# One gathered row in six is summed on GpSimd, with a descriptor ring of 4 KB

## The chip, the core and the metric

The kernel runs on one core of a Trainium2 chip. Its engines work side by side, each through its own queue in order: TensorE (PE in the profile, its weight loads PEld), VectorE (DVE), ScalarE (ACT), GpSimd (POOL) and SyncE (SP). Data moves between memory and the on-chip buffers through 16 DMA engines. The metric is the time of one execution on the device in microseconds (us).

## What is computed

Two layers of a decoder over 256 tokens of width 1024. Each layer mixes the tokens (four groups: short convolution, latent attention, conformer convolution, windowed attention), and then sends each token through PEER, a layer that picks 16 of 16384 experts for each of 8 heads. Cut to what matters here:

```python
def peer_ffn(x, w_q, sub_keys, u_tab, v_tab):
    ...
        gate = jax.nn.softmax(best_s, axis=-1).astype(xc.dtype)
        u = u_tab[idx]
        act = jax.nn.gelu(jnp.einsum('chkd,cd->chk', u, xc), approximate=False)
        vsel = v_tab[idx]
        return jnp.einsum('chk,chkd->cd', gate * act, vsel)

def reference(...):
    for l in range(DEPTH):
        ...
        h = layer_norm(ALPHA * x + mix @ w_out[l], ln1_g[l], ln1_b[l])
        x = layer_norm(ALPHA * h + peer_ffn(h, ...), ln2_g[l], ln2_b[l])
```

Every token needs 8 x 16 = 128 rows of u and of v, in float32; a row of u and one of v lie side by side in memory, 8 KB together.

## The kernel before

The tokens are two tiles of 128, one token to a partition. With two layers that makes four phases, (l, t) = (0,0), (0,1), (1,0), (1,1). A phase is the function `peer`: 128 steps k, one for each expert of a token. A step gathers one "row" tile (line 760: 128 tokens x 2048 floats, 1 MB, an indirect DMA issued by GpSimd into one of `ROWS` = 10 buffers), multiplies its u half with h and sums it up on VectorE (line 763, below "the product"), and the function `post` of the step before does the rest: gelu and gate on ScalarE (lines 745, 746), a 128x128 diagonal matrix `dg` from the result (line 748), and two matrix products of dg with the v half into `acc`, two PSUM banks that collect the sum over all 128 rows (line 750). When the last of these has read a row buffer, it is free for a later gather. `finish` adds ALPHA * h to acc (line 774) and does the layer norm.

While the rows of one phase run, other work is fed in between by `paced`: the mixer of the next tile (`mixer`, which ends with the products of w_out, line 585) and the routing that finds the experts of later heads (`route`). A step of `peer` is put out first, at high priority, then as much of the tasks as their share of `cost` says; `keep_behind` ties the tasks' instructions to steps a few slots back. So each engine has one fixed order in which row steps and tasks alternate. The last phase has no mixer beside it. Weights come through SyncE's queue (`load_w`); from the second mixer on, the four w_out pieces are loaded into row buffers (`w_out_rows` with a tile of tag "row"), which gathers can't use meanwhile.

Gathers land on eight semaphores that are used in turn, so the gather of row k+8 waits for the landing of row k, besides waiting for its buffer.

In the first mixer, 23 taps of a convolution are added on GpSimd (line 505), beside taps on VectorE (line 509).

Of the kernel before, what the change touches and what calls it, by code (L numbers as in the profile page):

```python
# [11 lines left out]
F32 = mybir.dt.float32  # L12
# [3 lines left out]
AF = mybir.ActivationFunctionType  # L16
ALU = mybir.AluOpType
AX = mybir.AxisListType

P = 128  # L20
DM = 1024
# [6 lines left out]
ALPHA = (2 * L) ** 0.25  # L28
# [20 lines left out]

ORDER0 = [1, 3, 0, 2]  # L50
ORDER = [3, 0, 2, 1]

TAPS = 24

# [10 lines left out]
def kernel(ctx: ExitStack, tc: tile.TileContext, x, positions, w_in, w_att, bcast, perch, lnrows, lncols,  # L65
                      w_out, w_qk, uv, ident, mla_mask, swa_dist, iota, invf, out):
    nc = tc.nc
    cp = ctx.enter_context(tc.tile_pool(name="cp", bufs=1))
    lp = ctx.enter_context(tc.tile_pool(name="lp", bufs=1))
# [9 lines left out]
    V, S = nc.vector, nc.scalar  # L79
# [62 lines left out]
    def layer_norm(dst, src, r, store=None, gb=None):  # L142

        mean, rstd = norm_stats(src, DM)
        yield 2.4
        for j in range(2):
            sl = slice(j * 512, (j + 1) * 512)
            if gb is not None:
                g, b = gb[:, sl], gb[:, DM + j * 512:DM + (j + 1) * 512]
            else:  # L150
                g, b = (pm.tile([P, 512], F32, tag="mm", name="lnp") for _ in range(2))
                for i, ps in enumerate((g, b)):
                    for k in range(4):
                        p = (r + i) * KC + j * 4 + k
                        nc.tensor.transpose(ps[:, k * P:(k + 1) * P], rows[:, p:p + 1].to_broadcast([P, P]), idn)
            V.scalar_tensor_tensor(src[:, sl], src[:, sl], mean, g, op0=ALU.subtract, op1=ALU.mult)  # L156
            V.scalar_tensor_tensor(dst[:, sl], src[:, sl], rstd, b, op0=ALU.mult, op1=ALU.add)
            if store is not None:
                nc.sync.dma_start(store[:, sl], dst[:, sl])
            yield 1.5  # L160
# [128 lines left out]
    def mixer(l, t, y, xt):  # L289
# [273 lines left out]
        hp = None  # L563
        order = ORDER0 if start else ORDER

# [168 lines left out]
        yield 0.5  # L734

    R, held, HT = {}, {}, {}

    def peer(l, t, h, acc):

        n = NH * TOPK  # L740
        order = HEADS[t]
        prev = None

        def post(k, act, row, gate):
            S.activation(act, act, AF.Gelu)  # L745
            S.activation(act, act, AF.Copy, scale=gate[:, k % TOPK:k % TOPK + 1])  # L746
            dg = gp.tile([P, P], F32, tag="dg", name="dg", bufs=3)
            S.activation(dg, idn, AF.Copy, scale=act)  # L748
            for j in range(2):
                nc.tensor.matmul(acc[j], dg, row[:, DM + j * 512:DM + (j + 1) * 512],  # L750
                                 start=(k == 0), stop=(k == n - 1))

        for k in range(n):
            while (l, t, order[k // TOPK]) not in R:
                yield None
            ix8, ix, gate = R[l, t, order[k // TOPK]]
            if ix8 is not None and k % TOPK < 8:
                ix = ix8
            row = gp.tile([P, 2 * DM], F32, tag="row", name="row")
            nc.gpsimd.indirect_dma_start(out=row, out_offset=None, in_=uv,  # L760
                                         in_offset=bass.IndirectOffsetOnAxis(ap=ix[:, k % TOPK:k % TOPK + 1], axis=0))
            act = gp.tile([P, 1], F32, tag="act", name="act", bufs=3)
            V.scalar_tensor_tensor(row[:, :DM], row[:, :DM], 1.0, h, op0=ALU.mult, op1=ALU.mult, accum_out=act)  # L763
            if prev is not None:
                post(*prev)
            prev = (k, act, row, gate)
            yield 1
        post(*prev)

    def finish(l, t, h, acc):  # L770
        hp = mp.tile([P, DM], F32, tag="S", name="hp2")
        for j in range(2):
            sl = slice(j * 512, (j + 1) * 512)
            V.scalar_tensor_tensor(hp[:, sl], h[:, sl], ALPHA, acc[j], op0=ALU.mult, op1=ALU.add)
        yield 1.2
        xo = xp.tile([P, DM], F32, tag="x", name=f"x{t}_{l}")
        yield from layer_norm(xo, hp, 4 * l + 2, out[t * P:(t + 1) * P, :] if l == L - 1 else None)
        X[t] = xo
# [175 lines left out]
```

## Time and profile before

| | before |
|---|---|
| time, median of 3 runs | 1524.01 us (1522.01 to 1524.16) |
| profiled execution, its own time | 1520.93 us |
| its span, first to last instruction | 1518.9 us |
| TensorE busy | 1336.2 us, 88% |
| VectorE busy | 1096.7 us, 72% |
| GpSimd busy | 632.3 us, 42% |
| ScalarE busy | 590.1 us, 39% |
| moved by DMA | 614.47 MB, mean 405 GB/s |

Busy times are shares of the whole span. Matrix products are pipelined, and a busy TensorE is not one at its peak. "DMA share" in the tables below is the mean share of time in which the 16 DMA engines had a packet in work; it comes out at up to 1.01 or 1.02. "Idle before" gives the time an engine waited ahead of an instruction, and what released it. The profiled execution is one run; its time lies 3.1 us below the median.

### The profile page before, as it was taken

What the parts mean: (1) busy time and instruction counts of PE and PEld (TensorE: products, weight loads), DVE (VectorE), ACT (ScalarE), POOL (GpSimd) and SP (SyncE); (2) the same over time, 40 slices, a digit from 0 to 9 for tenths busy, and PEclk for the clock granted to TensorE, in tenths of its full rate; (3) what the DMA queues carried; (4) which work ended last, traced back from release to release, by engine and by line L of the source; (5) the groups of instructions that cost most, each with busy time, mean ns of one, the idle gap of its engine ahead of it and who ended that gap; (6) DMA issues with size and microseconds to landing.
All of it is one profiled execution on the core that took longest, in us unless ns stands there. A gap on an engine that the chain in (4) does not pass through costs nothing.

```text
span 1518.9 us, 17527 instructions
## 1 busy us (share of the span) xinstructions
PE 1336.2 (88%) x4852; PEld 714.6 (47%) x4852; DVE 1096.7 (72%) x3161; ACT 590.1 (39%) x2047; POOL 632.3 (42%) x539
## 2 busy tenths in 40 slices
PE   8999979988989997889998989889998888888876
PEld 8576534444436653444445555544544433333222
DVE  5778887588767668876877667876887766676545
ACT  4233443334433324443343333542344334333332
POOL 2034333444554343444454333224355454655551
PEclk9999999999999999999999999899999999999999
DMA  9489999999999999999999999989999999999995
GB/s 383 177 324 426 426 428 396 385 401 424 426 426 427 426 426 427 420 389 426 427 427 426 427 426 427 411 334 407 419 426 428 426 427 426 427 427 427 427 427 220
DMA packets 86208, 614.47 MB, mean 405 GB/s; under 512 B 10336, under 2 KB 10720, under 8 KB 12768
## 3 DMA queue, kind: packets, MB, share of 16 engines
q0 software_dynamic: 73728, 536.90, 84.7%
q1 hardware_dynamic: 12096, 76.44, 12.3%
q8 instruction: 40, 0.66, 0.2%
q14 instruction: 56, 0.46, 0.1%
q10 hardware_dynamic: 288, 0.01, 0.0%
HBM read 612.26 MB, written 1.05 MB: 404 GB/s over the span
## 4 chain that ended last, share of the span: by engine, by line
PE 41%; DMA 31%; DVE 17%; ACT 5%; issue 4%; POOL 0%; DVEq 0%; POOLq 0%; SPq 0%; ACTq 0%
DMA row<-in_uv_dram,ix 31%; PE acc L750 24%; DVE row L763 7%; PE ps_q L680 6%; PE ps_o L585 3%; DVE cv L509 2%; ACT dg L748 1%; PE ps_cfa L319 1%; PE ps_mla L323 1%; ACT act L746 1%; PE ps_rs L685 1%; PE ps_scb L319 1%; ACT act L745 1%; PE po L284 1%; ACT L265 1%
## 5 line engine op out<-in xcount | busy, mean ns | idle before, releaser
L750 PE MATMUL acc<-row,dg 128*128 128x512 f32 x2048 | 977.9, 612 | 152.2 <-ACT dg L748 147.1
L760 POOL DMA_INDIRECT row<-in_uv_dram,ix x512 | 621.1, 1213 | 830.0 <-PE acc L750 272.5
L763 DVE SCALAR_TENSOR_TENSOR row<-row,h 128x1024 f32<-128x1024 f32 x512 | 619.2, 1219 | 217.2 <-DMA row<-in_uv_dram,ix 177.3
L750 PEld LDWEIGHTS acc<-row,dg 128*128 128x128 f32 x2048 | 364.1, 192 | 638.2 <-ACT dg L748 325.0
L745 ACT ACTIVATE act<-act 128x1 f32<-128x1 f32 x512 | 103.5, 202 | 586.2 <-DVE row L763 582.5
L748 ACT ACTIVATE dg<-idn,act 128x128 f32<-128x128 f32 x512 | 205.6, 402 | 24.8 <-PE acc L750 9.6
L746 ACT ACTIVATE act<-act,gate 128x1 f32<-128x1 f32 x512 | 150.2, 294 | 16.2 <-DVE gate L732 1.1
L680 PEld LDWEIGHTS ps_q<-hT,w_q_t 128*128 128x128 f32 x1024 | 124.1, 192 | 28.9 <-issue 27.3
L680 PE MATMUL ps_q<-hT,w_q_t 128*128 128x128 f32 x1024 | 126.9, 275 | 3.9 <-DVE hp L156 3.5
L509 DVE SCALAR_TENSOR_TENSOR cv<-cfu,pc,cv 128x128 f32<-128x128 f32 x217 | 67.6, 359 | 0.9
L585 PE MATMUL ps_o<-w_out_t,mT 128*128 128x512 f32 x128 | 60.9, 618 | 1.7 <-DVE mT L373 1.7
L655 DVE MAX8 tv<-rsc 128x8 f32<-128x128 f32 x64 | 18.5, 290 | 53.1 <-ACT rsc L687 47.5
L687 ACT COPY rsc<-ps_rs 128x128 f32<-128x128 f32 x64 | 17.0, 265 | 94.4 <-PE ps_rs L685 89.5
L683 ACT COPY rq<-ps_q 128x128 f32<-128x128 f32 x64 | 16.6, 259 | 66.2 <-PE ps_q L680 66.1
L763 DVE DVE_READ_ACCUMULATOR row<-row,h 128x1 f32 x512 | 42.2, 82 | 0.0
L585 PEld LDWEIGHTS ps_o<-w_out_t,mT 128*128 128x128 f32 x128 | 24.7, 198 | 31.0 <-issue 28.2
L685 PEld LDWEIGHTS ps_rs<-w_q_t,rq 128*128 128x128 f32 x128 | 22.9, 190 | 25.5 <-issue 20.9
L685 PE MATMUL ps_rs<-w_q_t,rq 128*128 128x128 f32 x128 | 24.7, 277 | 2.8 <-DVE hp L156 1.7
L323 PE MATMUL ps_mla<-w_in_t,xT 128*128 128x208 f32 x128 | 25.8, 353 | 0.6 <-ACT xT L118 0.5
L323 PEld LDWEIGHTS ps_mla<-w_in_t,xT 128*128 128x128 f32 x128 | 23.5, 199 | 3.9 <-issue 2.2
L649 DVE TENSOR_TENSOR grid<-tf,ab 128x512 f32<-128x512 f32 (+1 forms) x33 | 22.3, 674 | 0.6
L650 DVE TENSOR_REDUCE ex<-grid 128x32 f32<-128x512 f32 (+1 forms) x33 | 22.1, 671 | 0.6
(215 smaller groups left out, 958.7 us busy)
## 6 DMA issues: line engine op xcount, KB each, us to landing
w_in_t<-in_w_in_dram SPq DMA_DIRECT2D x24, 1024.0 KB, 9.5
w_q_t<-in_w_qk_dram SPq DMA_DIRECT2D x20, 1152.0 KB, 9.1
w_out_t<-in_w_out_dram SPq DMA_DIRECT2D x16, 1024.0 KB, 6.2
row<-in_uv_dram,ix POOLq DMA_INDIRECT x512
w_in_t<-in_w_in_dram SPq DMA_DIRECT2D x6, 832.0 KB, 8.7
att<-in_w_att_dram SPq DMA_DIRECT2D x2, 640.0 KB, 13.1
x<-in_x_dram SPq DMA_DIRECT2D x2, 512.0 KB
gb<-in_lnrows_dram SPq DMA_DIRECT2D x1, 1024.0 KB
```

Of the source, the lines that this page charges most:

```text
L319: nc.tensor.matmul(ps, w[:, c, j * P:(j + 1) * P], xT[:, c, :], start=(c == 0), stop=(c == KC - 1))
L323: nc.tensor.matmul(ps, xT[:, c, :], w[:, c, a:b], start=(c == 0), stop=(c == KC - 1))
L509: V.scalar_tensor_tensor(cv[j], src, wt, cv[j], op0=ALU.mult, op1=ALU.add)
L585: nc.tensor.matmul(po[j], mixed_T()[:, 2 * g + c, :], wg[:, c, j * 512:(j + 1) * 512], start=(n == 0 and c == 0), stop=(n == 3 and c == 1))
L680: nc.tensor.matmul(ps, wq[:, c, j * P:(j + 1) * P], hT[:, c, :], start=(c == 0), stop=(c == KC - 1))
L685: nc.tensor.matmul(ps, qT, w[:, KC * 256 + j * P:KC * 256 + (j + 1) * P], start=True, stop=True)
L745: S.activation(act, act, AF.Gelu)
L746: S.activation(act, act, AF.Copy, scale=gate[:, k % TOPK:k % TOPK + 1])
L748: S.activation(dg, idn, AF.Copy, scale=act)
L750: nc.tensor.matmul(acc[j], dg, row[:, DM + j * 512:DM + (j + 1) * 512], start=(k == 0), stop=(k == n - 1))
L760: nc.gpsimd.indirect_dma_start(out=row, out_offset=None, in_=uv, in_offset=bass.IndirectOffsetOnAxis(ap=ix[:, k % TOPK:k % TOPK + 1], axis=0))
L763: V.scalar_tensor_tensor(row[:, :DM], row[:, :DM], 1.0, h, op0=ALU.mult, op1=ALU.mult, accum_out=act)
```

## The change

In the phases (0,0), (0,1) and (1,0) each phase has a tile `side` of 128x1024. At step 5 ScalarE fills it with ALPHA * h. For the steps k = 9, 15, 21 and so on up to 123, `post` makes no dg and no matrix product: ScalarE scales the v half of the row in place (128x1024), and GpSimd adds it to `side`. `finish` then adds side and acc, in place of ALPHA * h and acc. The phase (1,1) stays as it was. The ring in which GpSimd writes the descriptors of its DMAs takes 4096 bytes of each partition; without the argument it takes 16384.

```diff
+SIDE = (6, 9)
...
+    SUM = {(0, 0): None, (0, 1): None, (1, 0): None}
...
+        aside = (l, t) in SUM
+
         def post(k, act, row, gate):
             S.activation(act, act, AF.Gelu)
             S.activation(act, act, AF.Copy, scale=gate[:, k % TOPK:k % TOPK + 1])
+            if aside and k >= SIDE[1] and (k - SIDE[1]) % SIDE[0] == 0 and k < n - 4:
+                v = row[:, DM:2 * DM]
+                S.activation(v, v, AF.Copy, scale=act)
+                nc.gpsimd.tensor_tensor(SUM[l, t], SUM[l, t], v, op=ALU.add)
+                return
             dg = gp.tile([P, P], F32, tag="dg", name="dg", bufs=3)
...
+            if aside and k == 5:
+
+                SUM[l, t] = lp.tile([P, DM], F32, tag="side", name="side")
+                S.activation(SUM[l, t], h, AF.Copy, scale=ALPHA)
             if prev is not None:
                 post(*prev)
...
-            V.scalar_tensor_tensor(hp[:, sl], h[:, sl], ALPHA, acc[j], op0=ALU.mult, op1=ALU.add)
+            if (l, t) in SUM:
+                V.tensor_tensor(hp[:, sl], SUM[l, t][:, sl], acc[j], op=ALU.add)
+            else:
+                V.scalar_tensor_tensor(hp[:, sl], h[:, sl], ALPHA, acc[j], op0=ALU.mult, op1=ALU.add)
...
-    nc = _bacc.Bacc("TRN2", target_bir_lowering=False, num_devices=1)
+    nc = _bacc.Bacc("TRN2", target_bir_lowering=False, num_devices=1, dynamic_dma_scratch_size=4096)
```

Lines of the kernel move with it: 750 becomes 760, 760 becomes 770, 763 becomes 773, 585 becomes 587; the new copy is line 754, the new add line 755.

GpSimd's order in the first phase, with the semaphores that each instruction waits for (DMASW0 to 7 are the landings of gathers; row_1204 is the row of k = 9, the last gather above the add is that of k = 17). Before:

```order
L760 DMA row_1358<-in_uv_dram,ix_1034 128x2048 [waits DMASW0_49,DVE_49,PE_49]
L760 DMA row_1399<-in_uv_dram,ix_1034 128x2048 [waits DMAHW4_49,DMASW1_49,PE_49]
L760 DMA row_1420<-in_uv_dram,ix_1034 128x2048 [waits DMASW2_49,DVE_49,PE_49]
L760 DMA row_1440<-in_uv_dram,ix_1034 128x2048 [waits DMASW3_49,DVE_49,PE_49]
L760 DMA row_1473<-in_uv_dram,ix_1034 128x2048 [waits DMASW4_49,DVE_49,PE_49]
```

The same place in the changed kernel:

```order
L770 DMA row_1358<-in_uv_dram,ix_1034 128x2048 [waits DMASW0_49,DVE_49,PE_49]
L770 DMA row_1397<-in_uv_dram,ix_1034 128x2048 [waits DMAHW4_49,DMASW1_49,PE_49]
L755 TENSOR_TENSOR side_1118<-side_1118,row_1204 128x1024 [waits Activation_49]
L770 DMA row_1418<-in_uv_dram,ix_1034 128x2048 [waits DMASW2_49,DVE_49,PE_49]
L770 DMA row_1438<-in_uv_dram,ix_1034 128x2048 [waits DMASW3_49,DVE_49,Pool_49]
L770 DMA row_1471<-in_uv_dram,ix_1034 128x2048 [waits DMASW4_49,DVE_49,PE_49]
```

The add of row k = 9 now stands between the gathers of k = 17 and k = 18 and waits for ScalarE; the gather of k = 19, which takes the buffer of k = 9, waits for GpSimd's own add in place of TensorE. The other 59 adds stand in much the same way, four to seven gathers apart from the next in most places.

TensorE's order near the end of the first phase's mixer, between the third and the fourth w_out group (ps_o). Before:

```order
L750 MATMUL acc_925<-row_2441,dg_2457 128x512
L750 MATMUL acc_926<-row_2441,dg_2457 128x512
L750 MATMUL acc_925<-row_2451,dg_2483 128x512
L750 MATMUL acc_926<-row_2451,dg_2483 128x512
L685 MATMUL ps_rs_2573<-w_q_t_2487,rq_2571 128x128
L750 MATMUL acc_925<-row_2477,dg_2505 128x512
L750 MATMUL acc_926<-row_2477,dg_2505 128x512
L750 MATMUL acc_925<-row_2499,dg_2516 128x512
L750 MATMUL acc_926<-row_2499,dg_2516 128x512
L750 MATMUL acc_925<-row_2510,dg_2535 128x512
L750 MATMUL acc_926<-row_2510,dg_2535 128x512
L585 MATMUL ps_o_2298<-w_out_t_2526,mT_1939 128x512 x2
```

The same place in the changed kernel:

```order
L760 MATMUL acc_925<-row_2425,dg_2441 128x512
L760 MATMUL acc_926<-row_2425,dg_2441 128x512
L687 MATMUL ps_rs_2555<-w_q_t_2469,rq_2553 128x128
L760 MATMUL acc_925<-row_2461,dg_2487 128x512
L760 MATMUL acc_926<-row_2461,dg_2487 128x512
L760 MATMUL acc_925<-row_2481,dg_2498 128x512
L760 MATMUL acc_926<-row_2481,dg_2498 128x512
L760 MATMUL acc_925<-row_2492,dg_2517 128x512
L760 MATMUL acc_926<-row_2492,dg_2517 128x512
L587 MATMUL ps_o_2284<-w_out_t_2508,mT_1931 128x512 x2
```

Five rows stood there and four stand there now; the routing product and the w_out group keep their places.

## Rows read from the trace of the kernel before

**Rows 1.** Busy time by stretch: span, engines (instructions), TensorE's clock, DMA share, GB/s.

```profile
88.00:228.00 140.00, 126.49 (x578) 78.86 (x576) 122.72 (x431) 60.24 (x208) 55.94 (x51) 0.98 0.99 418
228.00:361.00 133.00, 120.76 (x414) 62.54 (x415) 95.61 (x279) 47.66 (x174) 54.05 (x47) 1.00 0.99 398
361.00:608.00 247.00, 218.52 (x830) 121.14 (x829) 179.08 (x506) 96.75 (x338) 106.47 (x86) 0.98 1.01 426
608.00:684.00 76.00, 66.65 (x230) 34.63 (x229) 59.86 (x187) 34.88 (x120) 30.36 (x26) 0.96 1.00 404
684.00:969.00 285.00, 256.36 (x945) 139.82 (x944) 206.34 (x574) 109.31 (x380) 119.49 (x102) 0.98 1.01 426
969.00:1045.00 76.00, 69.82 (x255) 37.74 (x254) 58.76 (x192) 32.73 (x109) 22.70 (x23) 1.00 0.93 363
...
1121.00:1482.00 361.00, 309.01 (x840) 132.42 (x840) 241.56 (x562) 142.70 (x504) 196.51 (x148) 1.00 1.01 427
```

The engines in these rows are, in order, PE, PEld, DVE, ACT, POOL.

**Rows 2.** From the page: engines' busy time over the span, and GpSimd's DMA queue.

```profile
PE 1336.2 (88%) x4852; PEld 714.6 (47%) x4852; DVE 1096.7 (72%) x3161; ACT 590.1 (39%) x2047; POOL 632.3 (42%) x539
...
q0 software_dynamic: 73728, 536.90, 84.7%
```

**Rows 3.** The first gather (timeline: start, length), and line 763: ns min/median/max, first start.

```profile
88.39 1.09 POOL L760 DMA_INDIRECT row<-in_uv_dram,ix  x1 [52.20 <-issue]
...
L763 DVE SCALAR_TENSOR_TENSOR row<-row,h x512: 1194/1220/1301, 94.0 to 1504.9; 128x1024 f32<-128x1024 f32 x171
```

**Rows 4.** GpSimd's largest wait: 228 to 361, 608 to 684, 969 to 1045 us.

```profile
POOL row L760 <- PE acc L750: 27.5, 18, 3.2
...
POOL row L760 <- PE acc L750: 18.6, 11, 3.6
...
POOL row L760 <- PE acc L750: 19.6, 9, 5.6
```

**Rows 5.** From the page's costliest groups: busy us, mean ns, idle before.

```profile
L750 PE MATMUL acc<-row,dg 128*128 128x512 f32 x2048 | 977.9, 612 | 152.2 <-ACT dg L748 147.1
```

**Rows 6.** ScalarE's groups, each shape apart: busy us, mean ns, idle before.

```profile
L748 ACT ACTIVATE dg<-idn,act 128x128 f32<-128x128 f32 x512 | 205.6, 402 | 24.8 <-PE acc L750 9.6
L746 ACT ACTIVATE act<-act,gate 128x1 f32<-128x1 f32 x512 | 150.2, 294 | 16.2 <-DVE gate L732 1.1
L745 ACT ACTIVATE act<-act 128x1 f32<-128x1 f32 x512 | 103.5, 202 | 586.2 <-DVE row L763 582.5 <-issue 3.2
...
L118 ACT COPY xT<-ps_xT 128x512 f32<-128x512 f32 x5 | 2.9, 586 | 15.9 <-PE ps_xT L125 15.8
...
L451 ACT COPY sq<-ps_swq 128x256 f32<-128x256 f32 x4 | 1.4, 362 | 1.5 <-PE ps_swq L319 1.5
```

**Rows 7.** Small adds on GpSimd; VectorE's step beside them, then behind them (ns min/median/max).

```profile
L505 POOL TENSOR_TENSOR cv<-cv,tap x23: 454/457/621, 23.5 to 35.7; 128x128 f32<-128x128 f32 x23
...
L509 DVE SCALAR_TENSOR_TENSOR cv<-cfu,pc,cv x22: 352/499/607, 23.0 to 35.8; 128x128 f32<-128x128 f32 x22
...
L509 DVE SCALAR_TENSOR_TENSOR cv<-cfu,pc,cv x15: 345/348/353, 36.4 to 42.1; 128x128 f32<-128x128 f32 x15
```

**Rows 8.** Timeline of the steady state in the last phase: product, gather, next product.

```profile
1440.32 1.23 DVE L763 SCALAR_TENSOR_TENSOR row<-row,h 128x1024 f32<-128x1024 f32 x1 [1.24 <-DMA row<-in_uv_dram,ix]
...
1440.98 1.37 POOL L760 DMA_INDIRECT row<-in_uv_dram,ix  x1 [1.10 <-DMA row<-in_uv_dram,ix]
...
1442.76 1.23 DVE L763 SCALAR_TENSOR_TENSOR row<-row,h 128x1024 f32<-128x1024 f32 x1 [1.21 <-DMA row<-in_uv_dram,ix]
```

**Rows 9.** Timeline: two gathers beside VectorE's product, one behind its start, one ahead.

```profile
399.26 1.22 DVE L763 SCALAR_TENSOR_TENSOR row<-row,h 128x1024 f32<-128x1024 f32 x1
...
399.57 1.72 POOL L760 DMA_INDIRECT row<-in_uv_dram,ix  x1 [0.30 <-DVE tm L725]
...
403.40 0.94 POOL L760 DMA_INDIRECT row<-in_uv_dram,ix  x1 [0.30 <-issue]
...
403.47 1.23 DVE L763 SCALAR_TENSOR_TENSOR row<-row,h 128x1024 f32<-128x1024 f32 x1 [1.18 <-DMA row<-in_uv_dram,ix]
```

## The prediction

> **What bounds the kernel now.** I read the stage table first (busy time of each engine by stretch, with DMA share and GB/s), since a share over the whole span hides which stage is short of what. Between 361 and 608, 684 and 969, and 1121 and 1482 us the DMA engines are taken at a share of 1.01 and move 426 to 427 GB/s [rows 1]: a ceiling, held for 893 us while TensorE is busy 86 to 90% and VectorE 67 to 73%. TensorE's 88% of the span [rows 2] is therefore not the bound there: work taken off it in those stretches buys nothing. The reader is to look for the stretches below the ceiling. There are three behind the filling of the queue: 398 GB/s over 133 us, 404 over 76 us, 363 over 76 us [rows 1]. Against 427 they lose 29/427 x 133 = 9.0 us, 23/427 x 76 = 4.1 us and 64/427 x 76 = 11.4 us, together 24.5 us. Up to 88 us no gather runs [rows 3], and behind 1482 us the last rows drain; neither stretch is edited. So 24.5 us is about all that this edit can win, 1.6% of the time.
>
> Then I read the waits of GpSimd in these three stretches, because it issues the gathers: its largest is for TensorE's acc matmuls of line 750, 27.5, 18.6 and 19.6 us [rows 4]. That wait is for a row buffer. It fits the code: here the second half of the mixer borrows row buffers for w_out_t, and TensorE works through mixer, routing and row matmuls in one order.
>
> **The change, part by part.** Per phase k = 9, 15, ... 123 go aside: 20 rows, 60 in three phases.
>
> *Taken off TensorE.* One row's two products into acc appear as four MATMULs; 2048 of them are busy 977.9 us [rows 5], so 977.9/512 = 1.91 us a row, 60 x 1.91 = 115 us in all. What counts is what lies in the three stretches. They issue 47, 26 and 23 gathers or so (the instruction counts of POOL in [rows 1]), one in six aside: 8, 4 and 4, sixteen rows, 16 x 1.91 = 30.6 us. The excerpt from TensorE's order shows it: five rows between two w_out groups become four, and nothing else changes place. I count half of it, 15.3 us. TensorE is 91, 88 and 92% busy there [rows 1], so time taken from it does come forward, but part of it turns into waiting for the softmax and norm chains that the mixer runs on other engines.
>
> *Put on ScalarE.* A 128x128 dg (402 ns) gives way to a 128x1024 copy in place. Copies of 256 and 512 columns took 362 and 586 ns [rows 6], 0.875 ns a column; 402 + 896 x 0.875 = 1.19 us, so 0.79 us more a row, 47 us over 60 rows, and three begin-copies of 1.19 us. ScalarE is 36 to 46% busy in the three stretches [rows 1]; its free time hides this. Without that cover the next row's dg would come 0.8 us later.
>
> *Put on GpSimd.* The trace has GpSimd adds of 128x128 only: 457 ns [rows 7]. Were it all fixed cost, 128x1024 would take 0.46 us; were it all by column, 8 x 457 = 3.7 us. If as much of it is fixed as on VectorE (348 ns for 128 columns [rows 7], 1230 for 1024 [rows 8], so 222 ns fixed), 235 ns remain for 128 columns and the whole is 2.1 us. I take 2.5 us, between the last two and nearer to the one made from a step of the same kind.
>
> *The wait that comes with it.* In GpSimd's order the add of row k stands behind the gather of row k+8 and ahead of that of row k+9 (first excerpt). Queued behind it are all later gathers. Let row k's product on VectorE start at 0. In the steady state the gather of k+8 starts 0.66 us later, released by a landing, since eight landing semaphores are used in turn; the next is due 2.44 us on, at 3.1 us [rows 8]. The add can start when product, gelu, gate and copy are done, 1.2 + 0.2 + 0.3 + 1.2 and some gaps = 3.1 us [rows 6, 8], and ends at 5.6 us, or up to 6.8 us if it must first let a product pass. So one gather in six is 2.5 to 3.7 us late, and the two after it catch up, since a free gather takes 0.94 us [rows 9] and one is due each 2.44 us. Eight gathers of 2.44 us are some 19.5 us of work in hand, against 5.6 us from a first gather to its first product (88.4 to 94.0 us [rows 3]). So at the ceiling I cost this at nothing: the queue of landed and flying rows hides it. In the three stretches that queue is short and 3 us may show; but there the buffers are late already, and a row that goes aside no longer waits in TensorE's order. I set these two against each other.
>
> *VectorE against GpSimd.* This is the cost that can decide. In [rows 9] the gather of 399.57 us starts 0.31 us into a product of VectorE and takes 1.72 us; the one of 403.40 us starts 0.07 us ahead of a product and takes 0.94, the product 1.23 as ever. So the one that comes second waits. And while the 23 small adds ran, VectorE's two-input step over 128 columns took 499 ns, and 348 ns right behind them [rows 7]: 151 ns more for an add of 457 ns. By columns, 8 x 151 = 1.2 us a side row; below, nothing, if the add finds VectorE idle; above, the whole add, 2.5 us. I take 1.2 us: sixteen rows, 19 us of VectorE time in the three stretches. VectorE has 37, 16 and 17 us free there [rows 1] for 9.6, 4.8 and 4.8 us. I count a quarter as late in the first two (3.6 us) and all in the third (4.8 us), where the DMA engines fall furthest below the ceiling and a late product is felt at once. That is 8.4 us.
>
> The Trainium skill's page "SBUF — State Buffer", section "Who interferes with whom", speaks against this change: a VectorE instruction with two SBUF inputs and a GpSimd instruction that reads SBUF share a port pair, the pair is an exclusive lock, and whichever comes second is blocked until the first is done. The gathers agree with it; the small adds show a third of an add's length, not all of it. By the page's reading the 19 us would be 40 us.
>
> *The ring, and the rest.* A gather leaves 73728/512 = 144 packets [rows 2], 9 on each of 16 DMA engines, and the landing semaphores let eight gathers fly: 72 packets per engine. The trace has no ring size, so it cannot say when 4 KB is short; I cost it at nothing and keep a rival for it. The Trainium skill's "DMA: Bandwidth & Descriptors", section "Terms", gives a descriptor as 16 bytes; by that, and one descriptor a packet (an estimate), 4 KB would hold 256, and the sum would stay as it is; no run here shows it. The last step of a phase reads the side sum in place of h, the same shape: nothing.
>
> **The sum.** -15.3 + 8.4 = -6.9 us. The profiled execution took 1520.9 us (span 1518.9 and 2.0 around it): 1514.0. It lies 3.1 us below the median of the runs shown, so on the median: 1524.0 - 7 = **1517 us**.
>
> **The rivals.**
> (1) *The lock costs more than TensorE gives* (slower). The whole add blocks VectorE: 16 x 2.5 = 40 us in the three stretches. It decides once the blocking is above what VectorE has free around each add. Between 88 and 228 us VectorE has 140 - 122.7 = 17.3 us free [rows 1] for 7 adds, 17.5 us: just full. If half of the 40 us shows, +20 - 15 = +5, 1529 us; if all, 1549 us. For it: the gathers of [rows 9]. Against: the small adds of [rows 7], and VectorE's free fourth.
> (2) *No change.* The three stretches are short because the mixer holds buffers, not because TensorE is full; what TensorE saves it waits out. 1524 us. For it: other waits of GpSimd there, and the ceiling in the rest of the span. Against: [rows 4].
> (3) *All of the shortfall comes back*, since the relief, 30.6 us, is above the 24.5 us lost: 1499.5 us. Against: the third stretch loses 11.4 us and gets only 4 x 1.91 = 7.6 us.
> (4) *The ring is too small.* If it let only two gathers fly, a row would take 5.6/2 = 2.8 us in place of 2.44: 512 x 0.36 = 184 us more, about 1708 us. Against: [rows 2], 9 packets an engine.
>
> **How the numbers follow.** Forecast (a gain of 3 to 15 us) 0.46, rival 3 0.12, rival 2 0.18, rival 1 0.20, rival 4 0.04. Within 0.2%, 3 us, is about what a measurement of this kernel can't tell from no change. Faster 0.46 + 0.12 = 0.58, same 0.18, slower 0.24. For eight in ten I leave out the outermost part of rival 3, the upper end of rival 1 and rival 4: 1502 to 1533 us; below, 22 of the 24.5 us; above, 9 us, a little past rival 1 at half.
>
> **What would show it.** TensorE's busy time down by some 115 us (1336 to 1221) with the span almost the same is the plainest sign that it did not bound. The three stretches should show 402 to 415 GB/s; if one stays or falls and VectorE's products of line 773 there are longer or start later, rival 1 is at work. An add of 128x1024 should take 2.1 to 3.0 us; above 3.7 its cost was wrongly built up. If GB/s falls below 420 between 361 and 608 us, the late gathers are not hidden, or the ring is short; the waits of GpSimd tell which.

## Result, and the profile after

The changed kernel takes 1558.58 us (median of five runs, 1557.2 to 1561.01); the kernel before took 1522.01 us beside it (1516.62 to 1524.16). The ratio is 1.0244 with a 95% interval of 1.0229 to 1.026: 37 us slower. The forecast was 1517 us and the range ended at 1533. The profiled execution took 1561.01 us, with a span of 1559.2 us against 1518.9 before.

The stage table of the changed kernel: stretch, its length, busy time (and instructions) of PE, PEld, DVE, ACT and POOL, TensorE's clock, DMA share, GB/s. Its rows answer to [rows 1]; a row for 1045 to 1121 us is added.

```profile
88.00:228.00 140.00, 118.03 (x549) 75.25 (x547) 125.90 (x409) 56.85 (x187) 69.32 (x54) 0.94 0.98 402
228.00:361.00 133.00, 109.55 (x375) 57.65 (x376) 102.67 (x255) 56.37 (x181) 65.75 (x51) 0.92 0.94 375
361.00:608.00 247.00, 202.50 (x769) 114.16 (x767) 197.47 (x499) 102.20 (x332) 135.62 (x101) 0.93 1.01 420
608.00:684.00 76.00, 54.55 (x160) 28.68 (x160) 64.76 (x196) 35.02 (x102) 34.08 (x26) 0.80 0.94 356
684.00:969.00 285.00, 242.50 (x888) 133.69 (x889) 222.98 (x533) 115.59 (x373) 157.36 (x118) 0.95 1.01 422
969.00:1045.00 76.00, 55.83 (x205) 30.82 (x204) 62.68 (x215) 37.30 (x105) 26.75 (x22) 0.84 0.83 321
1045.00:1121.00 76.00, 68.71 (x249) 37.55 (x250) 58.18 (x134) 31.13 (x104) 43.98 (x34) 0.98 1.00 412
1121.00:1482.00 361.00, 301.50 (x844) 133.56 (x842) 264.40 (x628) 147.85 (x511) 210.44 (x153) 0.98 1.01 423
```

No stretch gained, every one lost. Against 427 GB/s the time lost is (427 - GB/s)/427 x length: 8.2, 16.2, 4.0, 12.6, 3.3, 18.9, 2.7 and 3.4 us, together 69.3. By the same sum the rows of before [rows 1] lose 2.9, 9.0, 0.6, 4.1, 0.7, 11.4, 0.7 (423 GB/s from 1045 to 1121 us) and nothing, together 29.4. The difference, 39.9 us, is the whole difference of the spans, 40.3 us. By these rows 23.2 us of it lie in the three stretches that the prediction wanted to shorten.

But the windows stand still while the program falls behind, by some 27 us at 969 us, so a line of this table is not the same work as its line of before. The stretches can be cut instead where the trace of the changed kernel has moved as many bytes as the kernel before at the edges of [rows 1]. Cut so, the first is 9.9 us longer than before and the three wanted ones 2.7, 11.4 and 9.6 us (23.7 together):

```profile
88.00:237.90 149.90, 122.41 (x557) 77.31 (x555) 133.74 (x427) 63.54 (x204) 72.99 (x57) 0.91 0.96 390
237.90:373.60 135.70, 111.63 (x382) 57.62 (x380) 107.26 (x280) 54.42 (x176) 69.94 (x55) 0.95 0.97 390
...
624.10:711.50 87.40, 67.64 (x217) 36.37 (x216) 70.92 (x194) 37.40 (x120) 42.26 (x31) 0.84 0.94 352
...
996.90:1082.50 85.60, 69.55 (x231) 36.22 (x231) 69.93 (x200) 38.82 (x119) 37.53 (x28) 0.90 0.85 322
```

The three at the ceiling (373.6 to 624.1, 711.5 to 996.9 and 1160.3 to 1521.9 us) are longer by 4.5 us together, and the one behind the third by 1.8. The kernel with the small ring alone (below), which has every instruction in the same place as the kernel before, differs from it by up to 3.2 us in one stretch by this measure; smaller differences of one stretch say nothing.

The page of the changed kernel: engines' busy time, then groups by line (count, busy us, mean ns of one, idle before and its releaser).

```profile
PE 1285.1 (82%) x4612; PEld 692.7 (44%) x4612; DVE 1193.9 (77%) x3161; ACT 636.2 (41%) x2050; POOL 779.4 (50%) x599
...
L760 PE MATMUL acc<-row,dg 128*128 128x512 f32 x1808 | 913.9, 640 | 239.7 <-ACT dg L758 236.0
...
L773 DVE SCALAR_TENSOR_TENSOR row<-row,h 128x1024 f32<-128x1024 f32 x512 | 666.7, 1315 | 158.9 <-DMA row<-in_uv_dram,ix 120.7
...
L755 POOL TENSOR_TENSOR side<-side,row 128x1024 f32<-128x1024 f32 x60 | 148.4, 2474 | 28.4 <-ACT row L754 25.1
...
L511 DVE SCALAR_TENSOR_TENSOR cv<-cfu,pc,cv 128x128 f32<-128x128 f32 x217 | 81.2, 420 | 0.9
L754 ACT ACTIVATE row<-row,act 128x1024 f32<-128x1024 f32 x60 | 68.9, 1148 | 3.1 <-issue 0.4
...
L657 DVE MAX8 tv<-rsc 128x8 f32<-128x128 f32 x64 | 18.5, 290 | 41.9 <-ACT rsc L689 39.0
```

Two of these lines in the kernel before:

```profile
L509 DVE SCALAR_TENSOR_TENSOR cv<-cfu,pc,cv 128x128 f32<-128x128 f32 x217 | 67.6, 359 | 0.9
...
L655 DVE MAX8 tv<-rsc 128x8 f32<-128x128 f32 x64 | 18.5, 290 | 53.1 <-ACT rsc L687 47.5 <-issue 5.6
```

VectorE executes the same 3161 instructions as before and is busy 97 us longer (1193.9 against 1096.7 [rows 2]): 1.62 us for each of the sixty adds. The product has a mean of 1315 ns, where it took 1220 before [rows 3]; the tap of line 511 has 420 ns, before 359. Both read two tiles from SBUF. MAX8, which reads one, stays at 290 ns.

The waits are seen in the timeline of the changed kernel (start, length, engine, line; GpSimd and VectorE, three places):

```profile
391.41 2.36 POOL L755 TENSOR_TENSOR side<-side,row 128x1024 f32<-128x1024 f32 x1
...
391.65 3.21 DVE L773 SCALAR_TENSOR_TENSOR row<-row,h 128x1024 f32<-128x1024 f32 x1 [1.39 <-issue]
...
1002.09 1.21 DVE L773 SCALAR_TENSOR_TENSOR row<-row,h 128x1024 f32<-128x1024 f32 x1
1002.67 2.85 POOL L755 TENSOR_TENSOR side<-side,row 128x1024 f32<-128x1024 f32 x1
...
1003.24 2.30 DVE L113 SCALAR_TENSOR_TENSOR rs_y<-rs_u,rs_y 128x1 f32<-128x1 f32 x1
...
1028.68 2.87 POOL L755 TENSOR_TENSOR side<-side,row 128x1024 f32<-128x1024 f32 x1 [0.25 <-ACT row L754]
1029.27 2.56 DVE L635 TENSOR_TENSOR grid<-tv 128x256 f32<-128x256 f32 x1
...
1031.82 0.95 POOL L770 DMA_INDIRECT row<-in_uv_dram,ix  x1 [0.27 <-DVE grid L635]
```

At 391 us the add is 0.24 us ahead of a product: it takes its 2.36 us, and the product ends 1.09 us after it, so about 2 us of its 3.21 are waiting. At 1002 us the add comes into a running product, waits half a microsecond and takes 2.85; then the next step of VectorE, a norm step over one column, lies for 2.30 us until the add is done. At 1029 us a step of the routing takes 2.56 us; the same step had a median of 414 ns over its 32 instances in this trace. The next gather stands behind the add in GpSimd's order and takes the buffer that an add frees; it goes out at 1031.82 us, 0.27 us behind the add. (The releaser that its line names is not what it waits for: the gather starts before that step ends.) The Trainium skill's page "SBUF — State Buffer", section "Who interferes with whom", says just this: a VectorE instruction with two SBUF inputs and a GpSimd instruction that reads SBUF exclude each other for a whole instruction. This trace agrees, 2.30 us for one column included.

How it reaches the end: GpSimd's largest wait from 228 to 361, from 608 to 684 and from 969 to 1045 us in the changed kernel (us in total, times, longest), to set beside [rows 4].

```profile
POOL row L770 <- PE acc L760: 25.0, 13, 4.2
...
POOL row L770 <- PE acc L760: 23.5, 10, 4.3
...
POOL row L770 <- PE acc L760: 40.4, 10, 9.3
```

It is still the acc products that gathers wait for, and in the last two stretches more than before (18.6 and 19.6 us), though TensorE has 240 of 2048 fewer of them. TensorE itself now sits idle 239.7 us ahead of line 760, mostly for dg, against 152.2 us [rows 5]. That fits the order of the code: a late product gives a late gelu, a late dg, a late acc product and a late buffer.

### The profile page after: what moved, and what is told of

Read it like the earlier page. It is cut to its first block, busy times and chain, and to the rows that moved or that the text cites. A ratio compares the mean times of both kernels' runs of the same rounds, so it can differ in the third digit from the quotient of the medians.

```text
span 1559.2 us, 17133 instructions
## 1 busy us (share of the span) xinstructions
PE 1285.1 (82%) x4612; PEld 692.7 (44%) x4612; DVE 1193.9 (77%) x3161; ACT 636.2 (41%) x2050; POOL 779.4 (50%) x599
## 4 chain that ended last, share of the span: by engine, by line
DMA 25%; PE 23%; DVE 21%; ACT 5%; issue 4%; POOL 1%; DVEq 0%; POOLq 0%; ACTq 0%
DMA row<-in_uv_dram,ix 25%; PE acc L760 15%; DVE row L773 10%; PE ps_q L682 3%; PE ps_o L587 1%; ACT dg L758 1%; ACT act L751 1%; ACT act L750 1%; DVE cv L511 1%; DVE ti L658 1%; DVE rsc L659 1%; DVE grid L651 1%; DVE ti L661 1%; ACT row L754 1%; POOL row L770 1%
## 5 line engine op out<-in xcount | busy, mean ns | idle before, releaser
L760 PE MATMUL acc<-row,dg 128*128 128x512 f32 x1808 | 913.9, 640 | 239.7 <-ACT dg L758 236.0
L773 DVE SCALAR_TENSOR_TENSOR row<-row,h 128x1024 f32<-128x1024 f32 x512 | 666.7, 1315 | 158.9 <-DMA row<-in_uv_dram,ix 120.7
L760 PEld LDWEIGHTS acc<-row,dg 128*128 128x128 f32 x1808 | 333.7, 200 | 697.4 <-ACT dg L758 411.1
L758 ACT ACTIVATE dg<-idn,act 128x128 f32<-128x128 f32 x452 | 181.6, 402 | 14.3 <-PE acc L760 0.6
L755 POOL TENSOR_TENSOR side<-side,row 128x1024 f32<-128x1024 f32 x60 | 148.4, 2474 | 28.4 <-ACT row L754 25.1
L511 DVE SCALAR_TENSOR_TENSOR cv<-cfu,pc,cv 128x128 f32<-128x128 f32 x217 | 81.2, 420 | 0.9
L754 ACT ACTIVATE row<-row,act 128x1024 f32<-128x1024 f32 x60 | 68.9, 1148 | 3.1 <-issue 0.4
```

The source lines that it names most:

```text
L511: V.scalar_tensor_tensor(cv[j], src, wt, cv[j], op0=ALU.mult, op1=ALU.add)
L754: S.activation(v, v, AF.Copy, scale=act)
L755: nc.gpsimd.tensor_tensor(SUM[l, t], SUM[l, t], v, op=ALU.add)
```

## The experiments

Every ratio is to the kernel before on the same chip, with its 95% interval. Four theories were open: VectorE's lost time (the "port theory" below); GpSimd's queue (gathers late behind an add of 2.4 us); TensorE's lower clock (0.939 over the run, 0.984 before); the ring.

Since an edit can move instructions in every engine's fixed order, the orders of the programs were set side by side (some 2500 instructions of TensorE, 2350 of VectorE, 2000 of ScalarE). Against the changed kernel, the one with the memset (below) has at most 5 in other places on any engine, and the one that only lacks the add at most 10. Against the kernel before, the one with the additional add has at most 3. These three pairs are clean. In most of the others some 20 to 230 instructions of VectorE lie elsewhere, and differences of some 10 us between such kernels can't be put down to the edit alone.

**The ring alone**, in the kernel before.

```diff
-    nc = _bacc.Bacc("TRN2", target_bir_lowering=False, num_devices=1)
+    nc = _bacc.Bacc("TRN2", target_bir_lowering=False, num_devices=1, dynamic_dma_scratch_size=4096)
```

> The kernel before with the descriptor ring of 4096 bytes and nothing else. If the ring holds back gathers, it should take most of the changed kernel's loss: 1545 to 1560 us, with GB/s below 427 between 1121 and 1482 us. If the ring has no part in it (my theory): 1522 us, within 3 us.

1523.58 us, ratio 1.0009 (0.9994 to 1.0024); the stretches from 361 to 608 and from 1121 to 1482 us move 427 GB/s. The ring has no part in it. (The third short stretch has 344 GB/s here, 363 in [rows 1], with the same order: so far can one stretch differ.)

**The changed kernel without the add.**

```diff
-                nc.gpsimd.tensor_tensor(SUM[l, t], SUM[l, t], v, op=ALU.add)
```

> The changed kernel without the add on GpSimd: the sixty rows are scaled on ScalarE and then left out of the sum. TensorE has the same relief and the same gaps. Port theory (VectorE's steps with two inputs wait out GpSimd's add): 1505 to 1522 us, VectorE's product back from 1315 to about 1220 ns in the mean. Clock theory (TensorE, with less to do, falls to its lower clock and this is the loss): 1545 us or more, granted clock about 0.94 as in the changed kernel. Queue theory (gathers stand behind the add in GpSimd's order): 1505 to 1522 us too.

1528.22 us, ratio 1.0052 (1.0032 to 1.0073). The product is back at 1219 ns and VectorE at 1096.5 us. So some 30 of the 37 us come with the add. The time is above the 1505 to 1522 us that both the port and the queue theory expected: the rest of the change, which takes sixty rows off TensorE, gains nothing and stands 5 to 11 us above the kernel before. The clock theory falls: the time is far from its 1545 us. Its page:

```profile
PE 1269.3 (83%) x4612; PEld 686.6 (45%) x4612; DVE 1096.5 (72%) x3161; ACT 635.7 (42%) x2050; POOL 638.6 (42%) x539
```

**The kernel before with an add beside it.** All rows go through TensorE; GpSimd adds every sixth row, as it landed, to a tile that nothing uses.

```diff
-                v = row[:, DM:2 * DM]
-                S.activation(v, v, AF.Copy, scale=act)
-                nc.gpsimd.tensor_tensor(SUM[l, t], SUM[l, t], v, op=ALU.add)
-                return
+                nc.gpsimd.tensor_tensor(SUM[l, t], SUM[l, t], row[:, DM:2 * DM], op=ALU.add)
...
-            if (l, t) in SUM:
+            if False:
```

> All rows go through TensorE as before, and GpSimd adds every sixth v row (unscaled) to the side sum as well, which nothing uses. Port theory: the loss is there in full or larger, 1550 to 1575 us, since nothing is taken off TensorE; VectorE's product about 1315 ns in the mean. Clock theory: TensorE keeps its work and its clock (0.98), so 1520 to 1530 us. Queue theory: the add waits for the row's landing only, not for ScalarE, so gathers are held up by some 2.4 us at most: 1522 to 1535 us.

1568.07 us, ratio 1.0325 (1.0296 to 1.0353): 47 us by the medians for the sixty adds alone, in the order of the kernel before. TensorE has all its work, and a clock of 0.973 in the profiled run; that doesn't save the time either. Its page:

```profile
PE 1350.8 (87%) x4852; PEld 723.9 (46%) x4852; DVE 1196.0 (77%) x3161; ACT 590.9 (38%) x2050; POOL 790.8 (51%) x599
...
L770 DVE SCALAR_TENSOR_TENSOR row<-row,h 128x1024 f32<-128x1024 f32 x512 | 668.2, 1317 | 165.3 <-DMA row<-in_uv_dram,ix 124.7
...
L753 POOL TENSOR_TENSOR side<-side,row 128x1024 f32<-128x1024 f32 x60 | 144.0, 2399 | 1.5 <-DMA row<-in_uv_dram,ix 0.3
```

The add waits for almost nothing here (1.5 us), and VectorE loses 99 us, 1.65 per add.

**A memset in place of the add.** It stands in the same place of GpSimd's queue and waits for the same copy, but only writes.

```diff
-                nc.gpsimd.tensor_tensor(SUM[l, t], SUM[l, t], v, op=ALU.add)
+                nc.gpsimd.memset(row, 0.0)
```

> The changed kernel with a GpSimd memset of the whole row (2048 columns) at the place of the add; the sixty rows are left out of the sum. It waits for the same copy, frees the row at the same point and holds the gathers behind it, but reads nothing. Its length is not known from a trace, I guess 1.5 to 2.5 us. Port theory (GpSimd's reads are what VectorE waits for): 1505 to 1525 us, product about 1220 ns. Queue theory: 1545 to 1560 us, as the changed kernel.

1525.97 us, ratio 1.0025 (1.0009 to 1.0041), a microsecond above what the port theory expected. From the page:

```profile
L773 DVE SCALAR_TENSOR_TENSOR row<-row,h 128x1024 f32<-128x1024 f32 x512 | 619.4, 1219 | 208.3 <-DMA row<-in_uv_dram,ix 167.9
...
L755 POOL MEMSET row<- 128x2048 f32 x60 | 109.0, 1817 | 26.7 <-ACT row L754 26.5
```

An instruction of 1.82 us between the gathers, with the same wait ahead of it (26.7 us here, 28.4 in the changed kernel), costs nothing that shows. With an order all but the same, the changed kernel is 33 us slower. The queue theory falls, but for the 0.66 us by which the add is longer than the memset; with VectorE's 86 us more, what costs is that the add reads.

**The add on VectorE.** If VectorE's time is the currency, an add made there should cost its share too.

```diff
-                S.activation(v, v, AF.Copy, scale=act)
-                nc.gpsimd.tensor_tensor(SUM[l, t], SUM[l, t], v, op=ALU.add)
+                V.scalar_tensor_tensor(SUM[l, t], v, act, SUM[l, t], op0=ALU.mult, op1=ALU.add)
```

> The side sum is kept on VectorE: one step with two inputs per side row (scale and add, 1024 columns) in place of ScalarE's copy and GpSimd's add. GpSimd has its gathers alone. If what was lost is VectorE's time, 99 us of it blocked by 60 adds in the changed kernel, then 60 x 1.22 = 73 us of work of its own should cost about three quarters as much: 1540 to 1553 us. If it is the blocking as such (products that wait at a bad moment, gathers behind them) and not the sum of VectorE's time: 1520 to 1532 us.

1541.79 us, ratio 1.0138 (1.0106 to 1.0169). One add takes:

```profile
L754 DVE SCALAR_TENSOR_TENSOR side<-row,act,side 128x1024 f32<-128x1024 f32 x60 | 76.8, 1280 | 46.8 <-ACT act L751 46.8
```

As expected, though the order is not the changed kernel's. VectorE (1160.9 us) is less busy than with GpSimd's help (1193.9). Against the kernel before, sixty adds of its own cost it 64 us, 1.07 each (an add takes 1.28 us and overlaps its neighbours a little); those on GpSimd cost it 97 us, 1.62 each, by waiting.

**The add in four pieces.**

```diff
-                nc.gpsimd.tensor_tensor(SUM[l, t], SUM[l, t], v, op=ALU.add)
+                for q in range(4):
+                    c = slice(q * 256, (q + 1) * 256)
+                    nc.gpsimd.tensor_tensor(SUM[l, t][:, c], SUM[l, t][:, c], v[:, c], op=ALU.add)
```

> The changed kernel with each add in four pieces of 256 columns, so that VectorE can get in between two of them. If the sum of the time that GpSimd holds VectorE off counts: 1555 to 1575 us, since four pieces read the same columns and pay a start each. If the length of one blocking counts, 1530 to 1545 us, and the longest product falls from 4.0 us to under 2.5.

1554.66 us, ratio 1.0222 (1.0187 to 1.0258): hardly better. The two lines by source (ns min/median/max, first and last start):

```profile
L757 POOL TENSOR_TENSOR side<-side,row x240: 711/739/1792, 125.8 to 1215.7; 128x256 f32<-128x256 f32 x120
...
L775 DVE SCALAR_TENSOR_TENSOR row<-row,h x512: 1196/1219/3655, 94.1 to 1537.0; 128x1024 f32<-128x1024 f32 x171
```

The longest product was to stay below 2.5 us and took 3.66: in the trace three pieces that start after it, at 774.41, 775.10 and 775.77 us, pass ahead of the product of 773.93. VectorE is busy 1172.2 us, 22 less than with whole adds, and the time is 4 us less, which the intervals don't tell from nothing.

**Sixty rows that end behind the gate**: no copy, no add.

```diff
-                v = row[:, DM:2 * DM]
-                S.activation(v, v, AF.Copy, scale=act)
-                nc.gpsimd.tensor_tensor(SUM[l, t], SUM[l, t], v, op=ALU.add)
                 return
```

> The run without the add, and without ScalarE's copy too: the sixty rows end with their gate and are left out of the sum; TensorE has the same relief. The run without the add was 7 us above the kernel before, not below. If the copy and the longer hold of the row made that, 1505 to 1522 us here. If TensorE's gaps and its lower clock made it, 1524 to 1532 us, with the granted clock again near 0.96.

1515.56 us, ratio 0.9957 (0.9941 to 0.9973). So much was gained where sixty rows cost TensorE nothing and free their buffers at their product: 7 us, in an order that has some 180 of VectorE's instructions elsewhere than the kernel before. Its third stretch rises to 391 GB/s from the 363 of [rows 1]:

```profile
969.00:1045.00 76.00, 67.33 (x223) 34.59 (x222) 57.93 (x184) 31.32 (x105) 29.56 (x26) 0.98 0.97 391
```

**The copy without the row.** ScalarE makes sixty copies of the same size from h, so that the row isn't held for them.

```diff
-                v = row[:, DM:2 * DM]
-                S.activation(v, v, AF.Copy, scale=act)
-                nc.gpsimd.tensor_tensor(SUM[l, t], SUM[l, t], v, op=ALU.add)
+                S.activation(SUM[l, t], h, AF.Copy, scale=act)
                 return
```

> The run without the add, with ScalarE's copy of 1024 columns taken from h into the side tile (scaled by the same act) in place of the row: ScalarE has the same 60 copies at the same places, but no row buffer is held for them, and the sixty rows are left out of the sum. With the copy on the row the time was 1528 us, without it 1516. If ScalarE's time and order made the difference: 1524 to 1531 us. If the row held longer made it: 1512 to 1519 us.

1513.18 us, ratio 0.9952 (0.9936 to 0.9967): as without a copy, with ScalarE busy 635.8 us in place of 570.5. ScalarE's time costs nothing that shows. The kernel without the add, whose copy is in the row, takes 15 us more. I first read this as the price of the held row; that doesn't go with the traces. From the end of its product to the end of the last instruction that reads its buffer a side row takes 2.7 us in the kernel without the add (mean of the sixty), and the same rows took 5.7 us in the kernel before, which is the faster one. The two kernels with the copies differ in the place of some 110 of VectorE's instructions, so the 15 us can come from the hold, from the order or from both.

**Eleven row buffers** in the kernel before, with the small ring that makes room for them.

```diff
-ROWS = 10
+ROWS = 11
```

> The kernel before with the small ring, and the room that it frees used for an eleventh row buffer (8 KB); no side sum. If the three stretches below the ceiling are short because w_out holds row buffers, they should gain: 1505 to 1516 us. If they are short of engine time, 1519 to 1525 us.

1519.67 us, ratio 0.9986 (0.997 to 1.0003): no difference that is certain. Two of its stretches, against 398 and 363 GB/s in [rows 1]:

```profile
228.00:361.00 133.00, 121.25 (x414) 63.59 (x413) 92.15 (x270) 47.88 (x172) 50.35 (x46) 0.98 0.96 385
...
969.00:1045.00 76.00, 74.69 (x274) 41.66 (x273) 63.95 (x218) 33.92 (x117) 30.03 (x28) 1.00 1.01 425
```

The third stretch is at the ceiling with TensorE's full work, far above the 344 and 363 GB/s of the two runs with ten buffers, whose order is the same: it was short of a buffer, not of TensorE. The first one lost 4 us, with some 160 instructions of VectorE in other places; why is open.

**Every twelfth row** in place of every sixth.

```diff
-SIDE = (6, 9)
+SIDE = (12, 9)
```

> The changed kernel with every twelfth row aside in place of every sixth, 30 rows in three phases. If each side row costs about the same, half of 37 us: 1536 to 1545 us. If there is a point above which VectorE runs out of free time, and half the rows stay under it: 1519 to 1530 us.

1538.7 us, ratio 1.0111 (1.0081 to 1.014), about half of the loss for half of the adds, as the first expectation had it:

```profile
L773 DVE SCALAR_TENSOR_TENSOR row<-row,h 128x1024 f32<-128x1024 f32 x512 | 646.1, 1272 | 194.0 <-DMA row<-in_uv_dram,ix 164.4
...
L755 POOL TENSOR_TENSOR side<-side,row 128x1024 f32<-128x1024 f32 x30 | 73.6, 2453 | 14.3 <-ACT row L754 12.8
```

With thirty adds or sixty, there is no sign of a free first part that VectorE's spare time would hide.

**The add without the copy.** GpSimd adds the row's product half right behind the product.

```diff
-                v = row[:, DM:2 * DM]
-                S.activation(v, v, AF.Copy, scale=act)
-                nc.gpsimd.tensor_tensor(SUM[l, t], SUM[l, t], v, op=ALU.add)
+                nc.gpsimd.tensor_tensor(SUM[l, t], SUM[l, t], row[:, :DM], op=ALU.add)
                 return
```

> The sixty rows skip TensorE and ScalarE's copy; GpSimd adds their product half (1024 columns, two inputs) to the side tile right behind VectorE's product, so the result is not the reference's. It has the relief (1516 us without any add) and the blocking of 60 adds, without the copy. If copy and blocking add up: 1516 + 30 = 1546 us, within 5. If the copy took part of what the blocking takes (the add put beside TensorE's full work cost 47 us): 1556 to 1564 us.

1554.01 us, ratio 1.0238 (1.0202 to 1.0274): 38 us by the medians, 43 by the ratios, over the kernel without copy and add, with 80 us more on VectorE (1175.6). The time lies between the two expectations and settles nothing between them.

**TensorE's work kept, no add.** For the sixty rows TensorE multiplies dg with h in place of the row, and the row is freed by ScalarE's copy.

```diff
-                nc.gpsimd.tensor_tensor(SUM[l, t], SUM[l, t], v, op=ALU.add)
-                return
+                src = h
+            else:
+                src = row[:, DM:2 * DM]
...
-                nc.tensor.matmul(acc[j], dg, row[:, DM + j * 512:DM + (j + 1) * 512],
+                nc.tensor.matmul(acc[j], dg, src[:, j * 512:(j + 1) * 512],
```

> The run without the add, with TensorE's work for the sixty rows put back, but on h in place of the row: dg and the two products as before, while the row buffer is freed by ScalarE's copy. The sixty rows are left out of the sum. Against the run without the add (1528 us, clock 0.96) only TensorE's relief is gone. If the relief was worth something there: 1531 to 1540 us. If it was worth nothing, or its gaps and the lower clock cost as much as it gave: 1519 to 1529 us, with the clock back at 0.98.

1526.93 us, ratio 1.0032 (1.0011 to 1.0054), and this is the page's line on the engines:

```profile
PE 1336.2 (88%) x4852; PEld 718.2 (47%) x4852; DVE 1096.7 (72%) x3161; ACT 654.0 (43%) x2110; POOL 638.2 (42%) x539
```

TensorE is as busy as before [rows 2], and the kernel is no slower than the one without the add, in which TensorE is relieved (1.0052, 1.0032 to 1.0073). So no worth of the relief is seen, with the lower clock that comes with it. But some 170 of VectorE's instructions have other places in the two, so a worth of up to some 10 us could hide there; that it is nothing is not shown.

Together: before to no add, +4 to +8 us (memset, no add); no add to the changed kernel, +30 to +33 us. No kernel that computes the whole was certainly faster than the one before.

## Why the prediction was wrong

**What bounds the kernel: right.** No stretch of any run is above 427 GB/s, and the losses against it add up to the difference of the spans.

**VectorE against GpSimd (+8.4 us): the step that failed.** It was sized as 16 rows x 1.2 us = 19 us on VectorE, a quarter late in two stretches and all in the third. The add brought 30 to 33 us (against the kernels without it and with the memset). Three parts of the term were too small.
- *The price.* 1.2 us came from the small adds of [rows 7] by columns. Measured: 86 us (memset to add), 97 us (before to after) and 99 us (the add beside the kernel before) for sixty, 1.4 to 1.65 us each. The value by columns was a sixth to a quarter too low; the upper bound, 2.5 us, is what one instruction suffers when it meets a whole add, and it does (2.30, 2.56 us).
- *The share that shows.* Sixteen adds fell into the three stretches, at 1.62 us each 26 us of VectorE's time, and 23.7 us more were lost there; 21 of them are the add's, since the kernel with the memset, cut in the same way, lost 2.6. So about four fifths show, where a quarter was assumed for two of the stretches. My reading, which no run tests by itself: VectorE's free time in a stretch is a sum of small gaps, and they don't stand where an add falls.
- *The rows not counted.* 44 of the sixty were left out because the ceiling hides them. Mostly it does: with 33 adds, the three stretches at the ceiling are 4.5 us longer. But the first stretch, of which the prediction itself had worked out that VectorE would be just full, is 9.9 us longer, against 4.5 with the memset.

Over the whole kernel 33 of 86 us show (memset to add), and 47 of 99 (before to additional add). Why the share is larger in the second, where TensorE has its full work, the runs don't tell. It leaves open that the relief is worth something once the adds are there: the changed kernel is 9 us faster than the one with the additional add (1558.58 and 1568.07 us), which also differs in the copy and in its order.

**Taken off TensorE (-15.3 us): failed too, and it gave the forecast its sign.** [rows 4] names TensorE's acc products as what gathers wait for, and that was taken for TensorE being full. In the same three stretches of the kernel before, TensorE itself sat idle ahead of its acc products, until ScalarE had made dg (us in total, times, longest):

```profile
PE acc L750 <- ACT dg L748: 13.8, 16, 2.3
...
PE acc L750 <- ACT dg L748: 6.4, 6, 3.2
...
PE acc L750 <- ACT dg L748: 3.4, 5, 1.1
```

So in the first stretch above all, the acc product was only the last link of a chain through dg, ScalarE and VectorE's product. Without the add the change costs 4 to 8 us; with TensorE's work kept it costs 5. With eleven buffers the third stretch is at 425 GB/s with TensorE's full work. That is rival 2's mechanism, buffers and not TensorE, shown for this stretch alone. No run gained more than 7 us, and that with side rows that are freed at their product.

**Rival 1 was the case, at its far end and beyond.** Its mechanism and place were right: products of line 773 became longer where GB/s fell. Its working let the add cost up to 40 us and took 15 us of relief off it, 1549 at most. The blocking brought 30 to 33 us, and the rest of the change, relief and all, 4 to 8 us more: 1558.6. It had a chance of 0.20 because the small adds of [rows 7] were set against the gathers of [rows 9], and the forecast sided with the small adds' price. The page of the Trainium skill that was cited against the change had the mechanism right; the prediction gave it its due as a rival, but not as the forecast.

**The copy on ScalarE (nothing): right for ScalarE.** 1148 ns where 1.19 us was worked out from [rows 6], and its time costs nothing that shows (the copy made elsewhere). What the prediction didn't have is that such an edit also moves VectorE's order and the buffers' release; kernels that differ in these lie from 7 us below to 8 us above the kernel before. Which of the two it is stays open.

**The add itself (2.5 us): right**, 2.36 us where nothing is in its way, 2.47 in the mean. **The gathers behind it (nothing): right**, by the memset. **The ring (nothing): right.**

**What would show it.** TensorE's busy time fell to 1285 us and not to 1221, though the 240 instructions are gone (4612 of 4852): those left run at a lower clock (640 ns in the mean, 612 before [rows 5]). The three stretches were to rise to 402 to 415 GB/s and fell to 375, 356 and 321, with longer products of line 773: the sign that the prediction gave for rival 1.

## What to carry to other kernels

When work goes to GpSimd that reads SBUF, count up to its whole length against VectorE, in every stretch, as long as VectorE is mostly in steps with two SBUF inputs (here 1.4 to 1.65 us of 2.47, with VectorE three quarters busy); then ask how much of VectorE's delay the kernel can hide, and don't take its free share of a stretch as room. An add on VectorE that raised its busy time by 1.07 us was cheaper than one on GpSimd that raised it by 1.62. And a wait that ends with an engine's instruction doesn't say that the engine is full: follow the chain one step back, to what that instruction itself was waiting for.

## What the runs showed of the hardware

- The exclusion has no regard for size: a step over one column waited 2.30 us for an add to end. It works both ways (adds of 2.36 us took up to 3.14 behind a product). MAX8, with one input, was untouched (290 ns), but not every step with one input was: tensor_scalar, one input and a constant, took up to 2.62 us beside an add (ns min/median/max):

```profile
L725 DVE TENSOR_SCALAR tm<-th x32: 155/175/2619, 95.8 to 1445.5; 128x16 f32<-128x16 f32 x32
```

- It isn't always the one that starts first in the trace that goes first. In the changed kernel this product starts 0.59 us ahead of the add, ends 1.08 us behind it, and takes 4.02 us:

```profile
642.37 4.02 DVE L773 SCALAR_TENSOR_TENSOR row<-row,h 128x1024 f32<-128x1024 f32 x1
642.96 2.35 POOL L755 TENSOR_TENSOR side<-side,row 128x1024 f32<-128x1024 f32 x1
```

- A memset of GpSimd, which reads nothing, has its own victims. By source (ns min/median/max), first with the memset, then without memset and add:

```profile
L725 DVE TENSOR_SCALAR tm<-th x32: 156/196/2244, 95.1 to 1410.6; 128x16 f32<-128x16 f32 x32
...
L727 DVE SCALAR_TENSOR_TENSOR tm<-th,tm x32: 155/174/196, 98.3 to 1411.3; 128x16 f32<-128x16 f32 x32
```

```profile
L725 DVE TENSOR_SCALAR tm<-th x32: 157/175/338, 94.3 to 1409.3; 128x16 f32<-128x16 f32 x32
```

  The step with one input and a constant takes up to 2.24 us beside the memset, the step with two inputs two lines on never more than 196 ns. The Trainium skill's page "SBUF — State Buffer", section "Who interferes with whom", gives tensor_scalar among the operations that can enter a two-port mode and then contend with GpSimd; this row agrees, with 2.24 us. VectorE's busy time is 11 us higher than without the memset (1107.9 against 1096.5), and none of it shows in the time (1525.97 us, 1528.22 without the memset). So 11 us of VectorE's time were lost for nothing here, where 86 us cost 33: it seems to depend on which step is late.
- TensorE's clock: from 608 to 684 us it is busy 54.6 of 76 us, 66.7 before, and the granted clock over the stretch is 0.80, where it was 0.96 before; from 969 to 1045 us it is busy 55.8 us, 69.8 before, at 0.84, 1.00 before. These are means over pieces at 2.4 and at 1.2 GHz. Over the whole run the clock is 0.939. The kernel without the add ran at 0.958 and the one with TensorE's work kept at 0.983, with times that can't be told apart (1528.22 and 1526.93 us). So the lower clock and the smaller work together come to nothing that shows; what the clock costs by itself, no run separates.
